# Sub-layer ends of a two-layer diffusion trunk: gate products and whole-tile splits on VectorE, two weight blocks of the first attention head in other tiles

## The chip, the core and the metric

One core of one Trainium2 chip runs the whole program. The metric is the device time of one execution in microseconds, lower is better. In the core, TensorE (PE) multiplies matrices, VectorE (DVE) and ScalarE (ACT) work on tiles of 128 partitions, GpSimd (POOL) does a few small or side operations, and SyncE (SP) issues the transfers. Each engine works through its own list of instructions in order and waits on semaphores for the others.

## The reference

A trunk of two layers on 256 context tokens and 512 latent tokens of width 1024. Each layer is a half-step SwiGLU FFN, a token mixer and another half-step FFN; layer 0 mixes by differential attention, layer 1 by grouped-query attention. Every one of these six sub-layers reads a normalised and modulated stream and adds its gated, normalised result back:

```python
def modulated_norm(h, g, m, k):
    return rmsnorm(h, g) * (1.0 + m[..., k + 1, :]) + m[..., k, :]

def gated_residual(h, y, g, m, k, weight):
    return h + weight * m[..., k + 2, :] * rmsnorm(y, g)

def half_ffn(h, m, k, g_pre, g_post, w_in, w_out):
    y = swiglu(modulated_norm(h, g_pre, m, k), w_in, w_out)
    return gated_residual(h, y, g_post, m, k, 0.5)
```

All is in float32. The output is the latent stream, 512 x 1024.

## The kernel before

**Numbers.** A float32 operand of TensorE is split into a high part `hi` (a cast on ScalarE) and a low part `lo = x - hi` (on VectorE), and a product is three matmuls: high-high, high-low, low-high. Activations live as `uh` and `ul` (high and low, transposed, the stationary operand), weights as `wh` and `wl`.

**Tiles.** The 768 tokens are six tiles of 128 tokens: 0 and 1 are context, 2 to 5 latent. `ys[t]` is the working tile of one token tile, 128 x 1024 in SBUF.

**The six sub-layers** run one after another: FFN (0,0) to about 545 us, differential attention to 1060, FFN (0,1) to 1540, FFN (1,0) to 2070, grouped attention to 2360, FFN (1,1) (latent tiles alone) to the end. Between two of them stands a sub-layer end: the last group of an output projection is summed tile by tile, and each finished tile is turned into the next sub-layer's input. I number the ends 1 to 6; ends 1, 3 and 4 close the FFNs (0,0), (0,1) and (1,0), ends 2 and 5 the two attentions, end 6 the kernel. The FFN ends work on six tiles, with five operands left for the last group: 30 matmuls a tile in two halves of 512 columns.

**One tile of an end** (class `Finish`) goes through: the sum from PSUM into `y` (`add_y`, L414, VectorE, once a half); the gate product `yg = y * gate` (`gated`, L369, GpSimd, once a half: half 0 from `half`, half 1 from `chain`); the sum of squares of `y` (L267, ScalarE); its inverse root on GpSimd (`rms`, two operations of 128 x 1, L97 and L99); `h = yg * r + h` (L382, VectorE), whose store is queued on SyncE; the sum of squares of `h` (L267) and its root (L97, L99); `y = h * r` (L388, VectorE); eight transposes on TensorE into `pre_t` (L280); the modulation back into `y` (L294 on VectorE, L290 on ScalarE, four pieces each); and the split, `split_u`: the cast `uh` on ScalarE (L310), then `ul = y - uh`. The table `WIDE` names 13 tiles over the first four ends that are split whole; there the low part is two halves of 128 x 512, one on VectorE (L315) and one on GpSimd (L316). All other tiles are split in two steps, each with its low half on VectorE (L318). At the attention ends `yg` and `h` are weight tiles, so the product reads there as `wh<-y,g` and `h` as `wl<-wh,rms,wl`.

**Order.** At the FFN ends the order of VectorE, ScalarE and GpSimd is the order in which `w_out_last` writes it (`ordered()`, with the table `LAGS` of how many halves each step of a tile trails the projection); on TensorE, and at the attention ends, a scheduler sets it, fed by the strings `DA_SLOT_END` and `GA_SLOT_END`. `marks` holds the last ACT, DVE and POOL instruction of a split or a root, and `behind` keeps the next FFN's loads of weights behind them.

**The first attention head.** Head 0 of differential attention needs eight k-blocks of `w_in`, loaded two by two by `block` (L846), cast (L849) and split (L852) into six `wh` and six `wl` weight tiles (`wtile`). At end 1 the output projection still holds five of the six. A block that is `kept` goes instead into two tiles of the tag `pl` (four buffers, idle there); before, that holds for the first block of heads 1, 3, 5 and 7.

Of the kernel before, what the change touches and what calls it, by code (L numbers as in the profile page):

```python
# [13 lines left out]
ALU = mybir.AluOpType  # L14
# [7 lines left out]
KC = D // P  # L22
# [32 lines left out]
def raw(ap):  # L55
    return ap.bitcast(F32)
# [3 lines left out]
def trunk(ctx: ExitStack, tc: tile.TileContext, a: dict, out: bass.AP):  # L60
    nc = tc.nc
# [44 lines left out]
    def stage():  # L106
        return wp.tile([P, 1024], F32, tag="stage", name="stage", bufs=NSTAGE)

    def wtile(which):
        return wp.tile([P, 1024], F32R, tag="w" + which, name="w" + which, bufs=6)  # L110
# [36 lines left out]
    marks = {}  # L147
# [155 lines left out]
    def split_u(t, place, parts):  # L303
        i, j = place
        u32 = ys[t].rearrange("p (k q) -> p k q", k=KC)
        n = KC // parts
        for k in range(0, KC, n):
            ks = slice(k, k + n)
            hi, lo = (x[:, i, ks, j * P : (j + 1) * P] for x in (uh, ul))
            marks["act"] = nc.scalar.copy(hi, u32[:, ks])  # L310
            if parts == 1:
                yield
            if parts == 1:
                m = KC // 2
                marks["dve"] = nc.vector.tensor_tensor(out=lo[:, :m], in0=u32[:, :m], in1=raw(hi[:, :m]), op=ALU.subtract)  # L315
                marks["pool"] = nc.gpsimd.tensor_tensor(out=lo[:, m:], in0=u32[:, m:], in1=raw(hi[:, m:]), op=ALU.subtract)  # L316
            else:
                marks["dve"] = nc.vector.tensor_tensor(out=lo, in0=u32[:, ks], in1=raw(hi), op=ALU.subtract)  # L318

    def load_gate(l, s):  # L320
        g = []
# [31 lines left out]
    class Finish:  # L353
# [10 lines left out]
        def gated(self, t, dh):  # L364

            if dh == 0:
                self.yg = self.tile()
            cols = slice(512 * dh, 512 * dh + 512)
            nc.gpsimd.tensor_tensor(  # L369
                out=self.yg[:, cols], in0=ys[t][:, cols], in1=self.gate[1 if t < CT else 0][:, cols], op=ALU.mult  # L370
            )

        def chain(self, t):
            i, j = self.place[t]
            cols = slice(j * P, (j + 1) * P)
            h = load_h(t, self.first, self.tile if self.s == 1 else None)
            ss = sumsq(ys[t], uh[:, i, :, cols])
            self.gated(t, 1)
            yg = self.yg
            r = rms(ss)  # L380
            yield
            nc.vector.scalar_tensor_tensor(out=h, in0=yg, scalar=r, in1=h, op0=ALU.mult, op1=ALU.add)  # L382
            nc.sync.dma_start(out=hd[t] if self.nxt else out[0, (t - CT) * P : (t - CT + 1) * P], in_=h)
            if not self.nxt:
                return
            r = rms(sumsq(h, ys[t]))
            yield
            nc.vector.tensor_scalar(out=ys[t], in0=h, scalar1=r, scalar2=None, op0=ALU.mult)  # L388
            yield
            pts = turn(t, t in self.wide)  # L390
            modulate(*self.nxt, t, [pts[k // 4][:, (k % 4) * P : (k % 4 + 1) * P] for k in range(KC)])
            yield
            yield from split_u(t, self.place[t], 1 if t in self.wide else 2)
# [416 lines left out]
    def diff_attention(ctx, place, fin):  # L810
# [22 lines left out]
        def block(n, parts, use, kept=False):  # L833


            def half(which):
                if kept:
                    return ep.tile([P, 768], F32R, tag="pl", name="w" + which, bufs=4)
                return wtile(which)[:, :n]

            st = stage()[:, :n]
            for cols, src in parts:
                dst = st[:, cols]
                if len(src.shape) == 3:
                    dst = dst.rearrange("p (c f) -> p c f", f=P)
                nc.sync.dma_start(out=dst, in_=src)  # L846
            yield
            hi = half("h")
            nc.scalar.copy(hi, st)  # L849
            yield  # L850
            lo = half("l")
            nc.vector.tensor_tensor(out=lo, in0=st, in1=raw(hi), op=ALU.subtract)  # L852
            use(hi, lo)
            yield

        class Head:
# [3 lines left out]
            def blocks(self):  # L860
                def use(k, hi, lo):
                    for i in range(2):
                        self.ws[k + i] = hi[:, i * 384 : (i + 1) * 384], lo[:, i * 384 : (i + 1) * 384]

                for k in range(0, KC, 2):
                    parts = [(slice(i * 384, (i + 1) * 384), w_in[:, k + i, :, self.h, :]) for i in range(2)]
                    yield block(768, parts, partial(use, k), k == 0 and self.h % 2)

            def open(self):
                self.q = {}  # L870
# [888 lines left out]
```

## Time and profile before

| what | before |
|---|---|
| time, median of 3 runs | 2739.59 us |
| lowest and highest run | 2735.0 and 2741.33 us |
| the profiled execution, own time | 2744.38 us |
| its span in the trace | 2742.6 us |
| mean granted TensorE clock, share of full speed | 0.988 |
| PE matmuls busy | 2639.0 us (96%) |
| DVE busy | 2016.4 us (74%) |
| ACT busy | 1135.7 us (41%) |
| POOL busy | 357.6 us (13%) |

The profiled execution is 4.8 us above the median and 1.8 us above its own span. "Busy" is the time in which an engine executes; matmuls are pipelined, so the ends of TensorE's rows are modelled. A row of a timeline begins with start and duration, and ends with the engine's idle time before the instruction and what released it.

### The profile page before, as it was taken

Reading aid. Unit: us, or ns where it says so; the run is one execution under the profiler, and the core shown is the slowest. Engines: PE = TensorE matmul, PEld = TensorE weight load, DVE = VectorE, ACT = ScalarE, POOL = GpSimd, SP = SyncE. Lnnn points to the kernel's source line nnn. Section 1 sums busy time; section 2 is a strip of 40 time slices with the busy share of each in tenths; the row PEclk is TensorE's granted clock in tenths of the full one; section 3 lists DMA queues with packets and bytes.
Section 4 is the critical chain, followed back from the end, with each engine's and each line's share of the span. In section 5 each row is a group of like instructions: output and inputs, shape, how many; then the busy total and the mean of one; then the engine's idle time right before and its main releaser. Section 6 shows DMA issues by size and latency. Waiting matters only on the chain.

```text
span 2742.6 us, 38868 instructions
## 1 busy us (share of the span) xinstructions
PE 2639.0 (96%) x14720; PEld 2404.6 (88%) x14720; DVE 2016.4 (74%) x3052; ACT 1135.7 (41%) x2323; POOL 357.6 (13%) x643
## 2 busy tenths in 40 slices
PE   6999999989999998999999999999999999899998
PEld 5999998879999987999988789999787899788887
DVE  4988879867777787888788689787766778733355
ACT  4333333156666665333342353333324554622232
POOL 0000000054333343000000310000004210200001
PEclk9999999999999999999999999999999999999999
DMA  7444457531111113444375334344743211444452
GB/s 229 136 132 151 142 170 254 167 122 45 38 32 49 54 63 97 134 124 139 117 251 175 123 104 154 125 137 155 282 141 131 79 39 39 149 142 139 149 166 89
DMA packets 301860, 354.13 MB, mean 129 GB/s; under 512 B 15808, under 2 KB 234088, under 8 KB 301672
## 3 DMA queue, kind: packets, MB, share of 16 engines
q1 hardware_dynamic: 301672, 351.64, 39.9%
q8 instruction: 116, 1.90, 0.3%
q14 instruction: 72, 0.59, 0.1%
HBM read 303.05 MB, written 48.54 MB: 128 GB/s over the span
## 4 chain that ended last, share of the span: by engine, by line
PE 75%; DVE 9%; ACT 5%; issue 5%; POOL 3%; DMA 2%; POOLq 0%; DVEq 0%; ACTq 0%; SPq 0%
PE y_ps L423 23%; PE ff_p L615 15%; PE ff_ps L615 12%; PE ff_ps L735 8%; PE qkv_ps L806 5%; PE ff_ps L477 2%; PE ff_ps L767 1%; DVE h L382 1%; PE S L984 1%; DVE wl L104 1%; PE o_ps L1056 1%; ACT y L267 1%; PE kv_ps L806 1%; PE q_ps L806 1%; PE o_ps L1428 1%
## 5 line engine op out<-in xcount | busy, mean ns | idle before, releaser
L423 PE MATMUL y_ps<-wh,gx 128*128 128x512 f32 x1936 | 604.5, 391 | 1.5 <-ACT wh L103 1.5
L423 PEld LDWEIGHTS y_ps<-wh,gx 128*128 128x128 f32 x1936 | 363.2, 188 | 81.1 <-ACT wh L103 2.9
L103 ACT CAST wh<-stage 128x1024 fp32r<-128x1024 f32 x224 | 232.1, 1048 | 434.7 <-PE y_ps L423 217.0
L423 PE MATMUL y_ps<-wl,gx 128*128 128x512 f32 x968 | 377.3, 390 | 0.5 <-DVE wl L104 0.4
L104 DVE TENSOR_TENSOR wl<-stage,wh 128x1024 fp32r<-128x1024 f32 x224 | 273.2, 1224 | 96.3 <-ACT wh L103 94.4
L414 DVE TENSOR_TENSOR y<-y_ps,y 128x512 f32<-128x512 f32 x324 | 221.3, 686 | 109.3 <-PE y_ps L423 107.7
L369 POOL TENSOR_TENSOR yg<-y,g 128x512 f32<-128x512 f32 x44 | 58.3, 1326 | 1820.3 <-DVE y L414 1818.1
L185 DVE SCALAR_TENSOR_TENSOR acc<-stage,scond,acc 128x1024 f32<-128x1024 f32 x196 | 244.1, 1277 | 30.3 <-DMA stage<-in_ada_w 30.2
L615 PE MATMUL ff_p<-t,wh 128*128 128x384 f32 x960 | 244.4, 335 | 1.5 <-ACT sil L568 1.5
L103 ACT CAST wh<-raw 128x1024 fp32r<-128x1024 f32 x120 | 120.1, 1049 | 255.9 <-DVE raw L594 255.9
L423 PEld LDWEIGHTS y_ps<-wl,gx 128*128 128x128 f32 x968 | 181.8, 188 | 38.5 <-DVE wl L104 1.6
L615 PEld LDWEIGHTS ff_p<-t,wh 128*128 128x128 f32 x960 | 173.8, 188 | 1.8 <-ACT sil L568 1.8
L615 PE MATMUL ff_p<-t,wl 128*128 128x384 f32 x480 | 161.0, 335 | 2.9 <-DVE wl L104 2.9
L615 PE MATMUL ff_ps<-uh,wh 128*128 128x384 f32 x480 | 160.9, 335 | 1.7 <-DVE two L637 1.7
L615 PE MATMUL ff_ps<-uh,wl 128*128 128x384 f32 x480 | 160.4, 334 | 0.0
L615 PE MATMUL ff_ps<-ul,wh 128*128 128x384 f32 x480 | 160.3, 334 | 0.0
L104 DVE TENSOR_TENSOR wl<-raw,wh 128x1024 fp32r<-128x1024 f32 x120 | 141.2, 1218 | 0.0
L806 PE MATMUL qkv_ps<-wh,uh 128*128 128x384 f32 x384 | 136.9, 357 | 4.1 <-ACT wh L849 2.7
L806 PE MATMUL qkv_ps<-wl,uh 128*128 128x384 f32 x384 | 129.8, 338 | 2.5 <-DVE wl L852 2.5
L615 PE MATMUL ff_p<-uh,u 128*128 128x384 f32 x480 | 132.1, 336 | 0.0
L806 PE MATMUL qkv_ps<-wh,ul 128*128 128x384 f32 x384 | 129.9, 338 | 0.1
L615 PE MATMUL ff_ps<-t,wh 128*128 128x384 f32 x480 | 124.6, 340 | 2.2 <-ACT one L633 1.9
(250 smaller groups left out, 6356.4 us busy)
## 6 DMA issues: line engine op xcount, KB each, us to landing
stage<-in_ffn_w_in SPq DMA_DIRECT2D x176, 512.0 KB
stage<-in_ada_w SPq DMA_DIRECT2D x136, 512.0 KB
stage<-in_ffn_w_out SPq DMA_DIRECT2D x88, 512.0 KB
gd<-g SPq DMA_DIRECT2D x66, 384.0 KB
gr<-gd SPq DMA_DIRECT2D x57, 384.0 KB
stage<-in_da_w_in SPq DMA_DIRECT2D x64, 192.0 KB
hd<-h SPq DMA_DIRECT2D x18, 512.0 KB
h<-hd SPq DMA_DIRECT2D x16, 512.0 KB
```

Source lines behind the costliest of these rows:

```text
L103: nc.scalar.copy(hi, src)
L104: nc.vector.tensor_tensor(out=lo, in0=src, in1=raw(hi), op=ALU.subtract)
L185: nc.vector.scalar_tensor_tensor(out=acc[c], in0=st, scalar=scond[:, k, c : c + 1], in1=acc[c], op0=ALU.mult, op1=ALU.add)
L267: nc.scalar.activation(junk, src, AF.Square, accum_out=ss)
L369: nc.gpsimd.tensor_tensor(out=self.yg[:, cols], in0=ys[t][:, cols], in1=self.gate[1 if t < CT else 0][:, cols], op=ALU.mult)
L382: nc.vector.scalar_tensor_tensor(out=h, in0=yg, scalar=r, in1=h, op0=ALU.mult, op1=ALU.add)
L414: nc.vector.tensor_tensor(out=y, in0=ps, in1=y, op=ALU.add)
L423: nc.tensor.matmul(ps, lhsT=x, rhs=w, start=(i == 0), stop=(i == n - 1))
L477: nc.tensor.matmul(ps, lhsT=ww[:, k, :], rhs=moving(uu, k, two), start=(k == 0 and n == 0), stop=(k == KC - 1 and n == 2),)
L615: nc.tensor.matmul(ps[:, :hw], lhsT=ww[:, k * P : (k + 1) * P], rhs=bb[:, k, cols], start=(first and k == 0 and n == 0), stop=(last and k ...
L735: nc.tensor.matmul(ps[:, :nt], lhsT=ww[:, k, :], rhs=uu[:, :, k, cols], start=(k == 0 and n == 0), stop=(k == KC - 1 and n == 2),)
L806: nc.tensor.matmul(ps[:, :n], lhsT=x, rhs=w, start=(k == 0 and m == 0), stop=(k == KC - 1 and m == 2))
```

## The change

Three things. The gate product `yg = y * gate` moves from GpSimd to VectorE, in all six ends (64 products of 128 x 512: 44 at the FFN ends, 20 at the attention ends). The low part of the 13 tiles that are split whole becomes one VectorE operation of 128 x 1024 in place of a half on VectorE and a half on GpSimd. And the first two blocks of head 0's `w_in` (k = 0 and k = 2, which hold k-blocks 0 to 3) become `kept`: they go into the four `pl` tiles, so that the third and the fourth block take the weight tiles that the first and the second had. The arithmetic is the same.

```diff
@@ split_u
-            if parts == 1:
-                m = KC // 2
-                marks["dve"] = nc.vector.tensor_tensor(out=lo[:, :m], in0=u32[:, :m], in1=raw(hi[:, :m]), op=ALU.subtract)
-                marks["pool"] = nc.gpsimd.tensor_tensor(out=lo[:, m:], in0=u32[:, m:], in1=raw(hi[:, m:]), op=ALU.subtract)
-            else:
-                marks["dve"] = nc.vector.tensor_tensor(out=lo, in0=u32[:, ks], in1=raw(hi), op=ALU.subtract)
+            marks["dve"] = nc.vector.tensor_tensor(out=lo, in0=u32[:, ks], in1=raw(hi), op=ALU.subtract)
@@ Finish.gated
-            nc.gpsimd.tensor_tensor(
+            nc.vector.tensor_tensor(
                 out=self.yg[:, cols], in0=ys[t][:, cols], in1=self.gate[1 if t < CT else 0][:, cols], op=ALU.mult
             )
@@ Head.blocks
-                    yield block(768, parts, partial(use, k), k == 0 and self.h % 2)
+                    yield block(768, parts, partial(use, k), k == 0 and self.h % 2 or k < 4 and self.h == 0)
```

The changed file is five lines shorter, so its line numbers are five lower from `load_gate` on (the product is L364 there, `add_y` L409, `h` L377, `y = h * r` L383, the split L313, the weight cast L844).

VectorE at end 3, one tile of the loop and the start of the next, before:

```order
L388 TENSOR_SCALAR y_103<-h,rms 128x1024
L414 TENSOR_TENSOR y_104<-y_ps,y_104 128x512
L315 TENSOR_TENSOR ul<-y_102,uh 128x4x128
L382 SCALAR_TENSOR_TENSOR h<-yg,rms,h 128x1024
L414 TENSOR_TENSOR y_105<-y_ps,y_105 128x512
L294 TENSOR_SCALAR y_103<-pre_t,ab_14976,ab_14316 128x128 x4
L388 TENSOR_SCALAR y_104<-h,rms 128x1024
```

and now:

```order
L409 TENSOR_TENSOR y_104<-y_ps,y_104 128x512
L364 TENSOR_TENSOR yg<-y_104,g_15576 128x512
L313 TENSOR_TENSOR ul<-y_102,uh 128x8x128
L377 SCALAR_TENSOR_TENSOR h<-yg,rms,h 128x1024
L409 TENSOR_TENSOR y_105<-y_ps,y_105 128x512
L364 TENSOR_TENSOR yg<-y_105,g_15576 128x512
L294 TENSOR_SCALAR y_103<-pre_t,ab_14971,ab_14311 128x128 x4
L383 TENSOR_SCALAR y_104<-h,rms 128x1024
```

Each sum of a half is now followed by its product, the split covers the whole tile, and nothing else changed places in the loop.

ScalarE where end 1 begins (`gx` and `wh` of L103 are the FFN's last operands, L849 or L844 the casts of head 0's blocks), before:

```order
L103 CAST gx<-gr 128x768
L103 CAST wh<-stage 128x1024
L849 CAST wh<-stage 128x768
L267 ACTIVATE uh,ss<-y_101 128x8x128
L267 ACTIVATE y_101,ss<-h 128x1024
```

and now:

```order
L103 CAST gx<-gr 128x768
L844 CAST wh<-stage 128x768
L103 CAST wh<-stage 128x1024
L844 CAST wh<-stage 128x768 x2
L267 ACTIVATE uh,ss<-y_101 128x8x128
L267 ACTIVATE y_101,ss<-h 128x1024
```

Three of head 0's four blocks are cast ahead of the first tile's sum of squares, where one was.

VectorE at end 5 (`neg`, `r` and `e` are steps of the attention's last units, y_103 is tile 2), before:

```order
L414 TENSOR_TENSOR y_103<-y_ps,y_103 128x512 x2
L1420 TENSOR_TENSOR pt<-p_t,pt 128x3x128 x2
L1389 TENSOR_REDUCE neg<-S 128x1
L382 SCALAR_TENSOR_TENSOR wl<-wh,rms,wl 128x1024
```

and now:

```order
L409 TENSOR_TENSOR y_103<-y_ps,y_103 128x512
L364 TENSOR_TENSOR wh<-y_103,g_23266 128x512
L409 TENSOR_TENSOR y_103<-y_ps,y_103 128x512
L1415 TENSOR_TENSOR pt<-p_t,pt 128x3x128
L364 TENSOR_TENSOR wh<-y_103,g_23266 128x512
L1415 TENSOR_TENSOR pt<-p_t,pt 128x3x128
L377 SCALAR_TENSOR_TENSOR wl<-wh,rms,wl 128x1024
L1384 TENSOR_REDUCE neg<-S 128x1
```

The scheduler has put two products among the attention's own work, and the maximum of a unit's scores (`neg`) behind `h` of tile 2.

## Rows read from the trace of the kernel before

**Rows 1.** The chain of work that ended last, shares of the span by engine:

```profile
PE 75%; DVE 9%; ACT 5%; issue 5%; POOL 3%; DMA 2%; POOLq 0%; DVEq 0%; ACTq 0%; SPq 0%
```

**Rows 2.** TensorE's waits, 525 to 640 us (total, times, longest, in us):

```profile
PE k_t L934 <- POOL ks L927: 3.0, 2, 2.1
PE qkv_ps L806 <- ACT wh L849: 2.7, 1, 2.7
PE qkv_ps L806 <- DVE wl L852: 2.5, 1, 2.5
PE pre_t L280 <- DVE y L388: 2.3, 2, 1.7
```

**Rows 3.** TensorE's waits, 1535 to 1612 us:

```profile
PE pre_t L280 <- DVE y L388: 2.8, 3, 1.7
```

**Rows 4.** TensorE's waits, 2055 to 2160 us:

```profile
PE k_t L1338 <- DVE xn L1286: 3.2, 1, 3.2
PE kv_ps L806 <- DVE wl L104: 2.6, 1, 2.6
```

**Rows 5.** TensorE's waits, 980 to 1085 us:

```profile
PE q_t L1081 <- DVE o L1078: 5.7, 3, 3.0
```

**Rows 6.** TensorE's waits, 2280 to 2400 us:

```profile
PE pre_t L280 <- DVE y L388: 3.5, 3, 1.3
PE ff_ps L477 <- DVE ul L318: 2.3, 1, 2.3
```

**Rows 7.** TensorE's timeline at end 1, the transposes of tiles 2 and 3:

```profile
571.11 1.09 PE L280 MATMUL pre_t<-ident,y 128*128 128x128 f32 x8 [0.54 <-DVE y L388]
...
580.77 1.09 PE L280 MATMUL pre_t<-ident,y 128*128 128x128 f32 x8 [1.74 <-DVE y L388]
```

**Rows 8.** VectorE's timeline at end 1:

```profile
547.92 1.29 DVE L382 SCALAR_TENSOR_TENSOR h<-yg,rms,h 128x1024 f32<-128x1024 f32 x1 [2.25 <-POOL rms L99]
...
564.72 2.31 DVE L382 SCALAR_TENSOR_TENSOR h<-yg,rms,h 128x1024 f32<-128x1024 f32 x1
...
569.28 1.77 DVE L388 TENSOR_SCALAR y<-h,rms 128x1024 f32<-128x1024 f32 x1 [0.36 <-POOL rms L99]
...
573.81 0.69 DVE L315 TENSOR_TENSOR ul<-y,uh 128x512 fp32r<-128x512 f32 x1 [2.16 <-ACT uh L310]
...
583.97 0.99 DVE L817 TENSOR_TENSOR lam<-lam 128x128 f32<-128x128 f32 x1 [2.65 <-DMA lam<-in_da_lambda]
...
601.36 0.75 DVE L388 TENSOR_SCALAR y<-h,rms 128x1024 f32<-128x1024 f32 x1 [0.77 <-POOL rms L99]
```

**Rows 9.** GpSimd's timeline at end 1:

```profile
564.16 1.80 POOL L316 TENSOR_TENSOR ul<-y,uh 128x512 fp32r<-128x512 f32 x1
...
568.37 0.22 POOL L97 TENSOR_SCALAR ms<-ss 128x1 f32<-128x1 f32 x1 [2.41 <-ACT y L267]
...
569.21 1.29 POOL L369 TENSOR_TENSOR yg<-y,g 128x512 f32<-128x512 f32 x1
...
594.64 0.93 POOL L97 TENSOR_SCALAR ms<-ss 128x1 f32<-128x1 f32 x1
```

**Rows 10.** VectorE by line and shape (busy us, mean ns | idle before, releaser):

```profile
L104 DVE TENSOR_TENSOR wl<-stage,wh 128x1024 fp32r<-128x1024 f32 x224 | 273.2, 1224 | 96.3 <-ACT wh L103 94.4
...
L382 DVE SCALAR_TENSOR_TENSOR h<-yg,rms,h 128x1024 f32<-128x1024 f32 x22 | 39.5, 1797 | 23.5 <-POOL rms L99 23.5
...
L388 DVE TENSOR_SCALAR y<-h,rms 128x1024 f32<-128x1024 f32 x18 | 28.7, 1594 | 13.1 <-POOL rms L99 13.1
...
L382 DVE SCALAR_TENSOR_TENSOR wl<-wh,rms,wl 128x1024 f32<-128x1024 f32 x10 | 12.8, 1279 | 4.2 <-POOL rms L99 4.2
...
L506 DVE TENSOR_TENSOR y<-y,y 128x512 f32<-128x512 f32 x9 | 6.1, 683 | 0.0
```

**Rows 11.** The last tile's `h` at end 3, VectorE's timeline:

```profile
1592.33 2.30 DVE L382 SCALAR_TENSOR_TENSOR h<-yg,rms,h 128x1024 f32<-128x1024 f32 x1
```

**Rows 12.** Busy us of each engine in a stretch of end 2 (PE, PEld, DVE, ACT, POOL):

```profile
960.00:1060.00 100.00, 86.00 (x497) 74.75 (x495) 81.89 (x154) 64.22 (x176) 50.49 (x88) 0.95 0.21 69
```

## The prediction

> **What bounds the kernel now.** The chain of waits comes first: three quarters of the span is TensorE's own work [rows 1], and the change touches none of it. So all that it can move is time in which TensorE stands still, and the next view is the list of TensorE's waits around each of the six ends. Each has the same picture: TensorE waits a few times for a tile on its way back from the sum to the next sub-layer's operand, or for that sub-layer's first weights. At the FFN ends (1, 3, 4) two waits of the transposes for `y = h * r` stand first (0.54 and 1.74 us at end 1 [rows 7]; at end 3 the same pair and one more, 2.8 us in all, 1.7 the longest [rows 3]); end 1 goes on with 2.7 us for a cast, 2.5 us for its low part and 2.1 us for the transposes of the first keys [rows 2]; end 4 with 2.6 us for a low part and 3.2 us for the keys [rows 4]. At the attention ends the waits hang on other steps: 5.7 us at end 2 on `o` of the last units [rows 5], 3.5 and 2.3 us at end 5 [rows 6]. End 6 has no such wait and one tile after another; there the product of a half runs beside ScalarE's sum of squares.
>
> Third, the timelines of VectorE and GpSimd at end 1, side by side. The same `h` takes 1.29 us at 547.92 and 2.31 us at 564.72 [rows 8], and beside the second runs GpSimd's half of a split, 564.16 to 565.96 [rows 9]: VectorE gets nowhere until GpSimd is through. The same holds for `y = h * r`: 1.77 us at 569.28 beside a product that began at 569.21, and 0.75 us at 601.36 with GpSimd idle [rows 8, 9]. Over the whole run the 22 `h` of the FFN ends and the tail average 1.80 us, the ten of the attention ends 1.28; the 18 `y` average 1.59 [rows 10]. So (1.80 - 1.28) x 22 = 11.4 us and (1.59 - 0.75) x 18 = 15.1 us of VectorE's time are such blocking, nearly all of it at ends 1, 3 and 4.
>
> **The FFN loop, step by step.** A tile there takes VectorE 9.66 us: the distance of the two transposes in [rows 7], of which TensorE itself needs 9.66 - 1.74 = 7.92. The loop runs sum, ScalarE's sum of squares and cast, low half, `h`, sum of squares, root, `y`, next sum. With nothing large left on GpSimd, `h` gives back 2.31 - 1.29 = 1.02 us and `y` 1.77 - 0.75 = 1.02. The split grows from a half (0.69 us [rows 8]) to a whole tile, for which the weight split of the same size stands, 1.22 us [rows 10]: +0.53. The two products cost VectorE 0.68 us each by the nearest row, a sum of two SBUF operands of 128 x 512 [rows 10]. The second starts when the sum is done and ends inside ScalarE's sum of squares of the same tile and its cast, for which VectorE now waits 2.16 us ahead of the split [rows 8]; the first lies between the sum of half 0 and the modulation, where VectorE has 0.36 us idle ahead of `y` [rows 8], so at most 0.68 - 0.36 = 0.32 of it shows. If the 2.16 us were not there, the pair would cost 1.36 a tile. New loop: 9.66 - 1.02 - 1.02 + 0.53 = 8.15 us, up to 8.5 with the 0.32. That is 0.2 to 0.6 over TensorE's 7.92. The first wait is 0.54 where the second is 1.74, so TensorE comes to it with 1.2 us in hand, which covers two to five such tiles: both transpose waits go, 2.3 us at each of the three ends.
>
> What is late next is the last tile. Its `h` is reached through three loops, three times -1.51, and is itself blocked (2.30 us at end 3 [rows 11]), another -1.0:
>
> End 3: -4.5 - 1.0 = **-5.5** us, taken from the last pair of tiles, for which the next FFN waits. All of TensorE's waits there end on this chain or go before it; -3.5 if the 0.32 and the sub-layer's first weights hold it, -6.5 if all of them vanish.
>
> End 4: two plain loops -3.0; in the last one the second product, a root step and VectorE's weight splits hold each other as at end 1 (a root's first step takes 0.93 us at 594.64 and 0.22 at 568.37 [rows 9]), which I put at -2.5; `h` -1.0; the keys' chain hangs on it. **-6.5**, from -4 to -8.5. The wait for the keys (3.2 us) stays in part, because TensorE gets there earlier too.
>
> End 1: loops into tiles 3 and 4, -3.0; the wait of VectorE for `lam` (2.65 us [rows 8]) does not shrink, since its transfer is queued on SyncE behind the store of an `h` that itself comes earlier; tile 4's `y` -1.0, tile 5's `h` -1.0, and the roots beside weight splits -1: **-6**. The new places of the weights matter here. In TensorE's order the first projections wait for the cast and the low part of head 0's second block, 2.7 + 2.5 us [rows 2]: these two blocks now lie in `pl` tiles and are cast ahead of tile 0's sum of squares, the third takes the one free weight tile. Those waits go whatever the loop does, but TensorE then runs on into the first key transposes, which need ScalarE to evacuate the first projection behind the sum of squares of tile 5's `h`. So the weights alone only move the wait, and the sum is what the last `h` gains. -3 if ScalarE's casts of the later blocks hold that `h`'s sum of squares, -9 if all waits of [rows 2] but the last go. The extra loads ahead of the first stores on SyncE are two blocks of 384 KB, early in a stretch with no transfer wait but `lam`; nothing.
>
> End 2: VectorE is busy 81.9 of 100 us [rows 12], the product is pure work there (the ten `h` of the attention ends are not blocked, 1.28 us [rows 10]). Twelve tiles' halves x 0.68 = 8.2 us come on VectorE; in return the roots of the attention's `o`, which hang behind products on GpSimd, come earlier, and that is the wait of 5.7 us [rows 5]. **-1**, from -4 to +2. End 5: eight halves x 0.68 = 5.4 us, the maximum of a unit's scores stands behind `h` of tile 2, 1.3 us later, against transposes and low parts freed of GpSimd's product [rows 6]: **+0.5**, from -3 to +2.5. End 6: 0.
>
> The Trainium skill, "Perfetto Trace Analysis", section Optimizing Scalar/DVE Operations, speaks for the other direction: when VectorE is saturated, work may be offloaded, even to GpSimd, though it "might not help" between these two. By it, end 2 would lose the 8.2 us of products in place of gaining 1; the trace at the FFN ends agrees with its reservation (2.31 against 1.29 us).
>
> **Sum.** -6 - 1 - 5.5 - 6.5 + 0.5 = -18.5, against the profiled execution's own 2744.4: 2725.9. That execution lies 4.8 above the median of the runs shown, so about 2721 on the scale of the median, 0.7% faster.
>
> **Rivals.**
> A, *only the loop waits go.* The three pairs of transpose waits vanish (2.3 + 2.3 + 2.3 = 6.9 us) and all that follows is caught by the next late thing: `lam` and ScalarE's queue at end 1, the keys at end 4, the first weights at end 3. For it: TensorE arrives earlier everywhere. Against: the keys' and the last pair's chains run through the very `h` and `y` that get shorter. With ends 2 and 5 at zero: 2739.6 - 6.9 = 2733.
>
> B, *VectorE becomes the bound at the attention ends*, slower than before. 20 products x 0.68 = 13.7 us go to an engine that is busy 82% there, in stretches in which its low parts and scores release TensorE. It decides if half of that or more lands on TensorE's waits at ends 2 and 5 and the FFN ends fare as in A, or worse, because products on VectorE now block GpSimd's roots (0.93 for 0.22 us, twice a tile, 0.7 x 2 x 4 tiles = 5.7 us at an end). With all 13.7 lost and 6.9 gained: 2739.6 + 6.8 = 2746.
> The Trainium skill, "SBUF — State Buffer", section Who interferes with whom, gives the lock behind this: an operation of VectorE with two SBUF inputs and a GpSimd operation that reads SBUF exclude each other, whoever issues first; by it a root can wait for a product of VectorE as `h` did for one of GpSimd, and the 0.93 us row is of that kind.
>
> C, *all waits at the FFN ends go*, with the stretches at half clock behind them: to the upper ends above, -9 - 4 - 6.5 - 8.5 - 3 = -31, 2709.
>
> D, *the weights' places backfire.* The four `pl` tiles are wanted again by head 1's first block and by the units of head 0; if head 1's block waits for the last projection of head 0, its cast comes too late for the next head. Price: one wait like the 2.7 + 2.5 us of [rows 2], +5 on the forecast: 2726.
>
> **How the numbers follow.** Forecast 0.62, C 0.08 (toward 2709), D 0.08 (2726), A 0.15 (2733), B 0.07 (2746). This kernel's measurement tells about 0.2%, 5.5 us, from no change: 2734.1 to 2745.1. Forecast, C and D are faster by more; A is faster in two cases of three, 0.10 against 0.05 within; B's 0.07 is split, 0.03 within and 0.04 slower. That makes 0.88, 0.08 and 0.04. The range leaves out C's far end and B: 2708 to 2734, the sums of the bounds (-31, and -3 + 2 - 3.5 - 4 + 2.5 = -6).
>
> **What would show it.** Right: every `h` at 1.28 and every `y` at 0.75 us in the loop, products of 0.68 us inside VectorE's wait for `uh`, no transpose wait at ends 1, 3 and 4, no wait for `wh` and `wl` at end 1, and a key wait there that is larger than before. Wrong: loops still above 9 us; roots on GpSimd near 1 us; TensorE's waits at ends 2 and 5 grown by more than 3 us each; a new wait for weights near 630 us, in head 1.

## The result and the profile after

| what | before | after |
|---|---|---|
| time, median | 2739.86 us | 2724.23 us |
| lowest and highest run | 2735.0, 2742.32 us | 2722.72, 2726.1 us |
| ratio, 95% interval | | 0.9941, 0.9931 to 0.9952 |
| the profiled execution, own time | 2744.38 us | 2724.36 us |
| its span | 2742.6 us | 2722.6 us |

The change is 15.6 us faster by the medians. The profiled pair differs by 20.0 us, more than the medians do; why is told below. The busy times of the page after:

```profile
PE 2632.1 (97%) x14720; PEld 2401.8 (88%) x14720; DVE 2026.2 (74%) x3116; ACT 1135.0 (42%) x2323; POOL 252.9 (9%) x566
```

GpSimd lost 105 us of work and VectorE gained only 10, though 44 us of products came to it: 26.5 us came back from `h` (39.5 to 28.2) and `y` (28.7 to 13.5). The rows by line and shape answer [rows 10] (busy us, mean ns of one | idle before, releaser):

```profile
L364 DVE TENSOR_TENSOR yg<-y,g 128x512 f32<-128x512 f32 x44 | 30.4, 692 | 1.3
L377 DVE SCALAR_TENSOR_TENSOR h<-yg,rms,h 128x1024 f32<-128x1024 f32 x22 | 28.2, 1282 | 15.9 <-POOL rms L99 15.9
...
L364 DVE TENSOR_TENSOR wh<-y,g 128x512 f32<-128x512 f32 x20 | 13.6, 685 | 0.1
L383 DVE TENSOR_SCALAR y<-h,rms 128x1024 f32<-128x1024 f32 x18 | 13.5, 749 | 6.5 <-POOL rms L99 6.5
```

`h` fell from 1797 to 1282 ns and `y` from 1594 to 749: nothing blocks them any more. TensorE's waits after, first end 1 (505 to 640 us), against [rows 2]:

```profile
PE k_t L929 <- POOL ks L922: 7.6, 2, 6.7
```

End 3 (1515 to 1612 us), against [rows 3]:

```profile
PE pre_t L280 <- DVE y L383: 1.8, 2, 1.1
```

End 4 (2035 to 2160 us), against [rows 4]:

```profile
PE k_t L1333 <- DVE xn L1281: 6.3, 1, 6.3
```

End 5 (2260 to 2400 us), against [rows 6]:

```profile
PE p_t L1403 <- DVE r L1394: 3.6, 1, 3.6
PE pre_t L280 <- DVE y L383: 3.5, 2, 2.5
```

The waits of the loop are gone at ends 1 and 4, and one wait for the keys holds most of what is left. At end 5 there is a wait that was not there before, 3.6 us for `r`.

**Shift by end.** How much an end gained is read from two traces: an instruction in the middle of a stage starts earlier by so much, and what the shift grows by from one stage to the next belongs to the end between them. Ahead of end 1 and behind it, before and then after:

```profile
518.29 0.69 DVE L414 TENSOR_TENSOR y<-y_ps,y 128x512 f32<-128x512 f32 x1 [0.41 <-PE y_ps L423]
...
704.04 0.90 ACT L1004 ACTIVATE e<-S,neg 128x768 f32<-128x768 f32 x1
```

```profile
517.14 0.69 DVE L409 TENSOR_TENSOR y<-y_ps,y 128x512 f32<-128x512 f32 x1 [0.41 <-PE y_ps L418]
...
697.93 0.90 ACT L999 ACTIVATE e<-S,neg 128x768 f32<-128x768 f32 x1
```

518.29 - 517.14 = 1.15 and 704.04 - 697.93 = 6.11: end 1 gained about 5. In the table each number is the median over 30 to 160 such pairs in a stage, always against the same trace of before; negative is earlier, in us. The kernels of the experiments stand in it too.

| kernel | end 1 | end 2 | end 3 | end 4 | end 5 | median time |
|---|---|---|---|---|---|---|
| before, a second trace | -0.1 | -1.1 | -0.3 | +0.1 | +0.1 | 2740.3 (1 run) |
| after | -5.1 | -2.0 | -7.1 | -8.4 | +3.8 | 2724.2 |
| after, a second trace | -3.9 | -1.3 | -6.5 | -8.6 | +3.8 | 2724.5 |
| split_only | -2.2 | -4.1 | -1.7 | -4.0 | +0.5 | 2731.9 |
| products_only | -3.3 | -0.1 | -4.2 | -5.6 | +3.4 | 2729.4 |
| blocks_only | +2.9 | -3.3 | -0.9 | -1.0 | +1.0 | 2740.3 |
| no_blocks | -4.6 | +0.5 | -6.5 | -7.7 | +1.3 | 2725.3 |
| end5_gpsimd | -4.2 | -1.7 | -6.5 | -8.4 | +0.8 | 2723.6 |
| end5_tile2 | -4.6 | -0.6 | -6.5 | -8.6 | +1.0 | 2722.8 |
| end2_gpsimd | -5.3 | -1.9 | -6.6 | -8.4 | +3.7 | 2722.9 |
| lam_later | -5.6 | -2.1 | -7.2 | -8.0 | +2.3 | 2723.2 |
| last_half_h | -7.0 | +1.1 | -5.5 | -9.6 | +2.2 | 2723.9 |
| combo2_h | -6.4 | -3.2 | -7.0 | -9.6 | -2.2 | 2718.4 |

The medians of before beside them lie between 2739.6 and 2740.5. The profiled execution of before is 4.5 us above its median of 2739.86 and that of after lies at its own, which is why the pair shows 20.0 and the medians 15.6. The second trace of before, near the median, shows where: it is 2.6 us earlier ahead of end 1 and 1.1 at end 2. Against that trace the ends of the changed kernel gain 17.5 us, not 18.8.

The column of end 3 holds more than end 3. Up to 1840 us the changed kernel has gained 5.9 us there, in both of its traces; the rest of the 7.1 and 6.5 comes near 1900 us, in the middle of FFN (1,0), where TensorE waits once for a weight. Before:

```profile
PE y_ps L423 <- ACT wh L103: 1.2, 1, 1.2
```

The changed kernel has no such wait in one trace and 0.6 us in the other.

### The profile page after: what moved, and what is told of

Same layout as the page of the kernel before. It is cut to its first block, busy times and chain, and to the rows that moved or that the text cites. A ratio compares the mean times of both kernels' runs of the same rounds, so it can differ in the third digit from the quotient of the medians.

```text
span 2722.6 us, 38903 instructions
## 1 busy us (share of the span) xinstructions
PE 2632.1 (97%) x14720; PEld 2401.8 (88%) x14720; DVE 2026.2 (74%) x3116; ACT 1135.0 (42%) x2323; POOL 252.9 (9%) x566
## 4 chain that ended last, share of the span: by engine, by line
issue 74%; PE 16%; DVE 4%; POOL 3%; ACT 3%; DMA 0%; POOLq 0%; DVEq 0%; ACTq 0%
PE qkv_ps L801 6%; PE y_ps L418 3%; PE S L979 1%; POOL rms L99 1%; PE o_ps L1051 1%; PE kv_ps L801 1%; PE q_ps L801 1%; PE o_ps L1423 1%; POOL ms L97 1%; ACT e L999 1%; PE S L1379 1%; POOL rs L91 1%; PE p_t L1031 1%; PE p_t L1403 0%; DMA h<-in_x 0%
## 5 line engine op out<-in xcount | busy, mean ns | idle before, releaser
L103 ACT CAST wh<-stage 128x1024 fp32r<-128x1024 f32 x224 | 232.3, 1049 | 427.7 <-PE y_ps L418 206.2
L409 DVE TENSOR_TENSOR y<-y_ps,y 128x512 f32<-128x512 f32 x324 | 222.1, 688 | 99.8 <-PE y_ps L418 98.3
L103 ACT CAST wh<-raw 128x1024 fp32r<-128x1024 f32 x120 | 120.1, 1049 | 256.5 <-DVE raw L589 256.5
L97 POOL TENSOR_SCALAR ms<-ss 128x1 f32<-128x1 f32 x66 | 22.8, 345 | 2050.8 <-ACT uh L267 1917.5
```

What stands on the lines that cost most here:

```text
L97: nc.gpsimd.tensor_scalar(out=ms, in0=ss, scalar1=D * EPS, scalar2=None, op0=ALU.add)
L103: nc.scalar.copy(hi, src)
L409: nc.vector.tensor_tensor(out=y, in0=ps, in1=y, op=ALU.add)
```

## The experiments

### The two halves of the change on GpSimd's work, one at a time

`split_only` is the kernel before with the whole-tile split alone:

```diff
...
-                m = KC // 2
-                marks["dve"] = nc.vector.tensor_tensor(out=lo[:, :m], ...)
-                marks["pool"] = nc.gpsimd.tensor_tensor(out=lo[:, m:], ...)
+            marks["dve"] = nc.vector.tensor_tensor(out=lo, in0=u32[:, ks], in1=raw(hi), op=ALU.subtract)
```

(The `if` and `else` around these lines go; tiles split in two steps keep their line.)

> The kernel before, with the whole-tile split on VectorE alone; products stay on GpSimd. Blocking theory: h is freed (1.28 us instead of 2.31 in the FFN loop), y = h * r stays blocked (1.77), the split costs 1.22 instead of 0.69, so a loop of 9.66 us becomes about 9.2. Shift of the trace by end: end 1 -2.5, end 3 -2.5, end 4 -3, ends 2 and 5 within 0.3 of zero; in all about -8 us, 2732. Rival, that what counts is how much is taken from GpSimd's list: 22 of the 108 us that left it would give about a fifth of the gain, -4.

`products_only` is the kernel before with the products alone:

```diff
-            nc.gpsimd.tensor_tensor(
+            nc.vector.tensor_tensor(
                 out=self.yg[:, cols], in0=ys[t][:, cols], in1=self.gate[...][:, cols], op=ALU.mult
...
```

> The kernel before, with the gate products on VectorE; the split stays in two halves. Blocking theory: y is freed (0.75), h stays blocked (2.31), loop about 8.6 us. End 1 -4, end 2 -2, end 3 -3, end 4 -4.5, end 5 +3.8 as in the changed kernel, in all about -10 us, 2730. Rival by the share of GpSimd's work: four fifths of the gain at the FFN ends, -16 there.

Measured: 2731.9 us, ratio 0.9969 (0.9957 to 0.9980), and 2729.4 us, 0.9962 (0.9949 to 0.9975), both times as expected. VectorE by line and shape, `split_only` and then `products_only`:

```profile
L383 DVE TENSOR_SCALAR y<-h,rms 128x1024 f32<-128x1024 f32 x18 | 28.8, 1598 | 13.6 <-POOL rms L99 13.6
L377 DVE SCALAR_TENSOR_TENSOR h<-yg,rms,h 128x1024 f32<-128x1024 f32 x22 | 28.2, 1282 | 23.8 <-POOL rms L99 23.8
```

```profile
L382 DVE SCALAR_TENSOR_TENSOR h<-yg,rms,h 128x1024 f32<-128x1024 f32 x22 | 39.5, 1797 | 16.3 <-POOL rms L99 16.3
L388 DVE TENSOR_SCALAR y<-h,rms 128x1024 f32<-128x1024 f32 x18 | 13.4, 746 | 5.6 <-POOL rms L99 5.6
```

Each part frees exactly the operation that it stood beside and leaves the other blocked: without GpSimd's half of the split `h` takes 1282 ns and `y` still 1598, without its products `y` takes 746 and `h` still 1797. At the three FFN ends the split gives 2.2 + 1.7 + 4.0 = 7.9 us and the products 3.3 + 4.2 + 5.6 = 13.1; both without the blocks give 4.6 + 6.5 + 7.7 = 18.8. The halves nearly add, 21.0 against 18.8. The rival, by the share of GpSimd's work, had put 4 and 16. So it is who stands beside whom that counts, more than how much GpSimd has to do. The -4.1 of `split_only` at end 2, where I had expected less than 0.3, is taken up below.

### The blocks, alone and left out

`blocks_only` has only the third part of the change, `no_blocks` all but it:

```diff
-                    yield block(768, parts, partial(use, k), k == 0 and self.h % 2)
+                    yield block(768, parts, partial(use, k), k == 0 and self.h % 2 or k < 4 and self.h == 0)
```

> The kernel before, with two blocks of head 0 in the pl tiles and nothing else. Theory, that the weights alone only move the wait: the waits for cast and low part (2.7 and 2.5 us) go, the wait for the first key transposes grows from 2.1 to about 7, end 1 within 0 to -1.5, no other end moves; 2738 to 2740. Rival, that the weights were the bound: end 1 -4 to -5, 2735.

> The changed kernel without the blocks in the pl tiles. Theory: end 1 loses 0 to 2 us against the changed kernel (its last h is what counts), the waits for cast and low part are back and the key wait is short; all other ends as in the changed kernel: 2724 to 2726. Rival, that the weights were the bound of end 1: +4 to +5, 2728 to 2729.

Measured: 2740.3 us, ratio 1.0002 (0.9993 to 1.0012), and 2725.3 us, 0.9942 (0.9925 to 0.9959). TensorE's waits from 525 to 640 us with the blocks alone, and below without them:

```profile
PE k_t L934 <- POOL ks L927: 5.9, 2, 5.1
...
PE qkv_ps L806 <- DVE wl L852: 2.5, 1, 2.5
PE qkv_ps L806 <- ACT wh L849: 0.6, 1, 0.6
```

```profile
PE k_t L929 <- POOL ks L922: 4.9, 2, 4.1
PE qkv_ps L801 <- DVE wl L847: 1.1, 2, 0.6
...
```

Alone, the blocks shorten the wait for a cast from 2.7 to 0.6 us, and the wait for the keys grows from 3.0 to 5.9 [rows 2]: the wait moves, and nothing is gained. I had expected both weight waits to go; the one for the low part stays at 2.5 us, and end 1 of this trace is even 2.9 us longer. Without the blocks, the waits for weights are only 1.1 us, which fits that they hung on the same loop; the keys wait 4.9 us there, where I had expected a short wait. The blocks bring nothing that these runs can tell from zero, alone or with the rest.

### The products at end 5

`end5_gpsimd` is the changed kernel with all eight products of end 5 back on GpSimd, `end5_tile2`, shown here, with only the two of tile 2:

```diff
-            nc.vector.tensor_tensor(
+            (nc.gpsimd if (self.l, self.s) == (1, 1) and t == CT else nc.vector).tensor_tensor(
```

> The changed kernel with the products of end 5 back on GpSimd. Order theory: the loss at end 5 comes from the scheduler's order, in which the maximum of a unit's scores stands behind h of tile 2; with the old order TensorE's wait of 3.6 us for r is gone and end 5 is back near the kernel before: 2 to 3.5 us less than the changed kernel, 2721 to 2723. Rival, that end 5's loss is only the clock (0.84 to 0.93 there in the changed kernel): no difference, 2724 to 2725.

> The changed kernel with only tile 2's two products of end 5 back on GpSimd; that alone puts the maximum ahead of h of tile 2 again. Order theory: the wait of 3.6 us for r is gone as with all eight products moved back, 2721 to 2723. Rival, that the load of eight products on VectorE is what costs: a quarter of the loss comes back, 1 us, 2723.5 to 2724.5, and the wait for r stays over 2.5 us.

Measured: 2723.6 us and 2722.8 us, ratios 0.9941 (0.9929 to 0.9954) and 0.9936 (0.9923 to 0.9950). VectorE's timeline of the changed kernel there, and TensorE's first transposes behind it:

```profile
2317.93 1.28 DVE L377 SCALAR_TENSOR_TENSOR wl<-wh,rms,wl 128x1024 f32<-128x1024 f32 x1 [0.77 <-POOL rms L99]
2319.13 0.95 DVE L1384 TENSOR_REDUCE neg<-S 128x1 f32<-128x768 f32 x1
...
```

```profile
2323.08 1.20 PE L1403 MATMUL p_t<-ident,e 128*128 128x128 f32 x5 [3.60 <-DVE r L1394]
```

and of `end5_tile2`, with its wait at that place:

```profile
2317.71 0.95 DVE L1384 TENSOR_REDUCE neg<-S 128x1 f32<-128x768 f32 x1
2319.17 1.28 DVE L377 SCALAR_TENSOR_TENSOR wl<-wh,rms,wl 128x1024 f32<-128x1024 f32 x1 [0.51 <-POOL rms L99]
```

```profile
PE p_t L1403 <- DVE e L1395: 0.8, 1, 0.8
```

With the maximum ahead of `h` the wait is 0.8 instead of 3.6 us, although six of the eight products are still VectorE's. So the wait hangs on the order, not on the load. In the traces end 5 drops from +3.8 to +1.0; the medians gain 0.6 to 1.7 us, which is inside what the runs scatter.

Part of that drop is TensorE's granted clock, the other explanation that I had named beforehand. Here are 140 us around end 5 at the same place in each trace (PE, PEld, DVE, ACT, POOL busy, granted clock): the changed kernel, `no_blocks`, `lam_later` (a run below) and `end5_tile2`. The first three have the changed kernel's wait of 3.6 us for `r`.

```profile
2256.20:2396.20 140.00, 128.69 (x795) 116.35 (x794) 100.62 (x180) 72.50 (x157) 10.81 (x22) 0.95 0.34 106
```

```profile
2259.00:2399.00 140.00, 128.21 (x805) 115.23 (x805) 100.72 (x181) 73.00 (x158) 10.84 (x22) 0.98 0.35 110
```

```profile
2256.35:2396.35 140.00, 128.41 (x801) 115.51 (x800) 100.59 (x180) 72.40 (x157) 10.81 (x22) 0.96 0.36 109
```

```profile
2257.40:2397.40 140.00, 129.96 (x807) 116.58 (x806) 99.77 (x179) 73.31 (x158) 13.40 (x24) 0.96 0.36 110
```

With the changed kernel's wait, end 5 stands at +3.8 where TensorE got 0.95 of its clock, at +2.3 with 0.96 and at +1.3 with 0.98. Without it, `end5_tile2` stands at +1.0 with 0.96, `end5_gpsimd` at +0.8 with 0.98, and the kernel before at 0 with 0.98. So at an equal clock the order costs 0.5 to 1.3 us; the rest of the 3.8 goes with the clock. Whether the wait for `r` itself brings the clock down stays open: six of the seven traces with that wait have 0.95 or 0.96, the five with all products of end 5 on GpSimd 0.98 or 0.99.

### The products at end 2

```diff
+            (nc.gpsimd if (self.l, self.s) == (0, 1) else nc.vector).tensor_tensor(
```

> The changed kernel with the products of end 2 back on GpSimd. Theory, that end 2 gains because the roots of o no longer queue behind products: the wait of 5.7 us on o is back (1.3 in the changed kernel), other waits of end 2 shrink by about 4, and the time is 0 to 2 us above the changed kernel, 2724 to 2726.5. Rival, that the products burden VectorE there: 2 us below, 2722.

Measured: 2722.9 us, ratio 0.9938 (0.9925 to 0.9950). TensorE's waits from 980 to 1085 us, the changed kernel and below it this one:

```profile
PE ff_ps L472 <- DVE wl L104: 4.3, 2, 2.4
PE ff_ps L472 <- ACT wh L103: 2.9, 2, 2.7
...
PE q_t L1076 <- DVE o L1073: 1.3, 1, 1.3
```

```profile
PE q_t L1076 <- DVE o L1073: 5.7, 3, 3.0
PE ff_ps L472 <- DVE wl L104: 3.4, 1, 3.4
```

The wait for `o` does come and go with the products, 5.7 against 1.3 us, as the theory says. But what it gives up is taken by the first weights of the next FFN (4.3 + 2.9 against 3.4), and the shift of end 2 is -1.9 here and -2.0 in the changed kernel. No gain and no loss can be told; the time lies below the 2724 to 2726.5 that I had expected.

### The kernels before and after, a second time

> The changed kernel once more, instruction for instruction, to see how far a single trace can be trusted: the waits by name and their lengths the same within 0.1 us, the shift of an end against the earlier trace of the same kernel up to 1 us at the FFN ends, and up to 2.5 us at ends 2 and 5, where the granted clock fell to 0.8 or 0.9 in some traces of one and the same order and not in others. Time 2724 to 2725.

> The kernel before once more, for a second trace to hold the ends of the others against. If end 2 of the changed kernel is really 1 to 2 us shorter, this trace keeps end 2 within 1 us of the first; the rival is that end 2 moves by 2 to 4 us from trace to trace of one and the same order, as the trace with only the blocks moved suggests (-3.3 there, with nothing changed at end 2), and then nothing below that is to be told at end 2. FFN ends within 1 us of the first trace.

Measured: 2724.5 us, ratio 0.9941 (0.9929 to 0.9954); one run of before, 2740.3 us. By name and length its waits at the ends are those of the first trace within 0.4 us, and its end 1 differs by 1.2; I had put 0.1 and 1. End 2 moved by 1.1 us between the two traces of before, and `blocks_only`, with nothing changed at end 2, `split_only`, with one tile's split changed there, and `no_blocks`, with end 2 as in the changed kernel, stand at -3.3, -4.1 and +0.5. A shift of 2 us at end 2 is no finding.

### What is late next

`lam_later` is the changed kernel with VectorE's steps on `lam` behind the last `y` of end 1 (`scaled[0]` is that instruction). The transfer of `lam` and ScalarE's exponential, whose table load takes 1.28 us in the loop of the changed kernel, stand later with them:

```diff
+        with tc.issue_after(scaled[0].ins):
+            lp = lam[:, 4:6]
+            nc.vector.tensor_tensor(out=lp, in0=lam[:, 0:4:2, :], in1=lam[:, 1:4:2, :], op=ALU.mult)
...
```

> The changed kernel with VectorE's work on lam, for which it waits 2.3 us in the loop of end 1, put behind the last tile's y. Theory, that the last h of end 1 sets its length: the key wait of 6.7 us falls to about 4 and end 1 is 2 to 3 us shorter, 2721 to 2723. Rival, that ScalarE's casts of late weight transfers hold the keys: no difference, 2724 to 2725.

`last_half_h` puts the last tile's second sum and its `h` first:

```diff
-                stages(2 * (t - start) + dh)
+                e = 2 * (t - start) + dh
+                if t < tiles[-1]:
+                    stages(e)
+                elif dh:
+                    stages(e - 1)
+                    if stage_of[t] == 1 and t in coming:
+                        step(t)
+                    stages(e)
```

> The changed kernel with another order at the end of the FFN ends: the last tile's second sum stands ahead of tile 4's scaling and tile 3's modulation on VectorE, and its h ahead of tile 3's split. Theory, that after the change the last h is what the next sub-layer waits for: the key waits of 6.7 and 6.3 us at ends 1 and 4 shrink by 2 to 3 each (at end 1 the wait for lam and late weight casts keep the rest), end 3 has only 2.2 us of waits left and gives 1 at most; in all -6, 2717 to 2720. Rival, that the keys hang on ScalarE's casts: under 2 us in all, 2722.5 or more.

`combo2_h` is both, `end5_tile2`, and the casts of the next head behind the last `y` of end 1:

```diff
-        whole(3)
+        with tc.issue_after(scaled[0].ins):
+            whole(3)
```

> The changed kernel with all that the runs so far point to: the last tile's sum and h first, lam and the next head's casts behind the last y of end 1, tile 2's products of end 5 on GpSimd. If the parts add: end 1 -4.5, end 3 -1, end 4 -3, end 5 -1.5 against the changed kernel, 2714 (2711 to 2717). Rival, that TensorE's granted clock takes back what the waits give: 2718 or more.

Measured: 2723.2 us, ratio 0.9940 (0.9927 to 0.9952); 2723.9 us, 0.9934 (0.9922 to 0.9946); 2718.4 us, 0.9923 (0.9909 to 0.9936). The wait for the keys at end 1, in that order:

```profile
PE k_t L919 <- POOL ks L912: 5.9, 2, 5.1
```

```profile
PE k_t L936 <- POOL ks L929: 5.7, 2, 4.9
```

```profile
PE k_t L926 <- POOL ks L919: 5.3, 2, 4.4
```

They take 1.6 to 2.3 us off the changed kernel's longest wait of 6.7; for each of the first two I had put 2 to 3. The shift of end 1 is -5.6, -7.0 and -6.4, against -5.1 and -3.9 in the changed kernel. ScalarE in `lam_later` shows a part of what holds the rest: a cast that waits for its transfer, ahead of the sum of squares of the last `h`.

```profile
590.92 0.83 ACT L834 CAST wh<-stage 128x768 fp32r<-128x768 f32 x1 [1.50 <-DMA stage<-in_da_w_in]
591.66 1.05 ACT L267 ACTIVATE y<-h 128x1024 f32<-128x1024 f32 x1
```

That `h` ends at 591.14 (589.86 and 1.28), so the cast costs 0.5 us; no run takes the other 4.6 apart.

The time of `last_half_h` is the rival's, under 2 us in all, though ends 1 and 4 do gain in its trace (-7.0 and -9.6, against -5.1 and -8.4). At end 3, where tile 4's `y` now stands behind tile 5's sum and product, the new order makes a wait of its own:

```profile
PE pre_t L280 <- DVE y L383: 2.8, 1, 2.8
```

against 1.8 us in the changed kernel. `combo2_h` has the lowest median of all kernels here, 6 us below the changed one; its interval and the changed kernel's overlap (0.9936 and 0.9931). It misses the 2711 to 2717 that I had expected and lies where the rival had it, that the clock takes back what the waits give. Its trace cannot show that: it is of the fastest run (2713.9), and its -2.2 at end 5, with the order of `end5_tile2`, goes with a clock of 0.99 against 0.96.

## Why the prediction was right, point by point

The time, 2724.2, lies in the range, 3 us above the 2721 that was forecast.

**The blocking.** Right, and shown by the two halves: `h` 1282 and `y` 749 ns, products 692.

**The loop.** Put at 8.15 to 8.5 us; VectorE's timeline of the changed kernel at end 1, two tiles of it:

```profile
561.84 1.22 DVE L313 TENSOR_TENSOR ul<-y,uh 128x1024 fp32r<-128x1024 f32 x1 [1.62 <-ACT uh L310]
562.98 1.28 DVE L377 SCALAR_TENSOR_TENSOR h<-yg,rms,h 128x1024 f32<-128x1024 f32 x1
...
566.79 0.75 DVE L383 TENSOR_SCALAR y<-h,rms 128x1024 f32<-128x1024 f32 x1
...
570.49 1.23 DVE L313 TENSOR_TENSOR ul<-y,uh 128x1024 fp32r<-128x1024 f32 x1 [1.63 <-ACT uh L310]
571.63 1.28 DVE L377 SCALAR_TENSOR_TENSOR h<-yg,rms,h 128x1024 f32<-128x1024 f32 x1
...
579.84 0.29 DVE L812 TENSOR_TENSOR lam<-lam 128x128 f32<-128x128 f32 x1 [2.34 <-DMA lam<-in_da_lambda]
```

571.63 - 562.98 = 8.65 us, 0.15 over the upper bound: of the 0.36 us that VectorE idled ahead of `y` nothing is left, so the first product shows, as the 0.32 said. The second hides in the wait for `uh`, 1.62 now where it was 2.16. All transpose waits at ends 1 and 4 are gone, and at end 3 1.8 of 2.8 us remain, where none was to.

**End 1, -6.** The first key transposes start at 603.54 before and 596.48 after; less the 1.15 of the opening that is -5.9. Behind them the end gives back 0.8, and over the two traces it is -5.1 and -3.9. The wait for `lam` stayed (2.65 and 2.34 us), and the blocks alone gave nothing, both as put. That the two waits for weights go "whatever the loop does" was wrong: with the blocks alone 2.5 us stay, and the loop without the blocks leaves only 1.1. And the bound of -9 does not follow from [rows 2]: without the keys the waits there add up to 7.5.

**End 3, -5.5.** Right: -5.9 up to 1840 us, in both traces; only with the wait near 1900 does the table's -7.1 pass the bound of -6.5. The last `h`, to be held against [rows 11]:

```profile
1579.70 1.28 DVE L377 SCALAR_TENSOR_TENSOR h<-yg,rms,h 128x1024 f32<-128x1024 f32 x1
```

It starts 12.63 us earlier, of which 8.26 had been gained by then: -4.4, where three loops were put at -4.5. TensorE's waits at this end, 6.3 us in all before, are 2.2 after. The rest of the gain fits its clock, which the sum had left out. In the 20 us around the last tile it was granted 0.91 before and 1.00 after, which is 1.8 us by an estimate from these two rows:

```profile
1580.00:1600.00 20.00, 16.58 (x113) 15.46 (x112) 14.32 (x21) 10.19 (x20) 9.31 (x13) 0.91 0.31 107
```

```profile
1565.50:1585.50 20.00, 18.19 (x130) 16.70 (x129) 15.91 (x26) 12.71 (x26) 3.71 (x8) 1.00 0.31 106
```

**End 4, -6.5**, measured -8.4 and -8.6, at the bound of -8.5. The keys of end 4, before and after:

```profile
2129.90 0.45 PE L1338 MATMUL k_t<-ident,xn 128*128 128x128 f32 x1 [3.21 <-DVE xn L1286]
```

```profile
2107.86 0.45 PE L1333 MATMUL k_t<-ident,xn 128*128 128x128 f32 x1 [6.26 <-DVE xn L1281]
```

22.04 us earlier, of which 15.39 had been gained by then: -6.65, the step as it was worked out. Its parts were not: the last `h` starts 4.5 us earlier, where 5.5 had been put, and the way from it to `y` is 2.2 shorter, where 1.0 had been put. The other 1.8 us come behind the keys. In the same 20 us (2130.00 to 2150.00 before, 2107.96 to 2127.96 after) TensorE was granted 0.86 of its clock before and 0.91 after, by the same estimate 1.0 us, and two of its waits there shrink from 2.3 to 1.7 us.

**End 2, -1**: not to be told from zero. The step on the roots is right (5.7 to 1.3 us), but I had not asked what is late next there, as I had at the FFN ends.

**End 5, +0.5**, bound +2.5: measured +3.8 twice. This is the term that was mis-sized. I had read the order, and priced the maximum's place at the 1.3 us of `h` and set it against gains; but the row of `h` brings its own wait for a root with it, two maxima then run back to back behind it, and `r` and `e` of both units follow them, so that TensorE waits 3.6 us. That wait replaces others: all of TensorE's waits at this end grow from 9.7 to 11.3 us, and at the clock of before (0.98) the same order stands at +1.3, inside the bounds. What takes it past them is the clock of 0.95, which the sum had left out here too.

**Sum.** Ends -5.1 - 2.0 - 7.1 - 8.4 + 3.8 = -18.8 in the profiled pair, forecast -18.5; -16.5 in the second trace, and -15.6 by the medians. Gains at ends 3 and 4 and the loss at end 5 made up for each other, and in all three a part is TensorE's clock, up there and down here. That the sum comes so near is partly luck; the blocking and the loop are no luck.

**The rivals.** A (the waits only move, -6.9): at end 1 most of the wait did turn up at the keys, but earlier, and the time is 9 us below A's 2733. B: its mechanism is real at one place. At end 4 a root's first step, GpSimd's timeline of the changed kernel, and VectorE beside it:

```profile
2098.75 2.88 POOL L97 TENSOR_SCALAR ms<-ss 128x1 f32<-128x1 f32 x1 [3.21 <-ACT uh L267]
```

```profile
2098.06 2.36 DVE L104 TENSOR_TENSOR wl<-stage,wh 128x1024 fp32r<-128x1024 f32 x2
...
2100.33 1.22 DVE L313 TENSOR_TENSOR ul<-y,uh 128x1024 fp32r<-128x1024 f32 x1
```

All over the run, though, the 66 such steps average 345 ns after and 325 before (22.8 against 21.5 us): 1.3 us, not 5.7 an end; and ends 2 and 5 together lost 1.8 us, not 13.7. C: the waits at the FFN ends did not all go; the keys still wait 6.7 and 6.3 us. D: no wait for weights near 630 us.

## What to carry to other kernels

Look at the operations of two engines that stand beside each other, not at the engines' totals: here a product of 1.3 us on GpSimd, busy 13%, made the `y` beside it on VectorE 1.0 us longer, 15 times of 18, on the chain that mattered. Price an end by following the last tile through it, and ask at every end what is late next; and where a scheduler has put a step behind another, price the wait that this other step brings with it, not its duration alone. Before an end of one trace is held against that of another, compare the granted clock.

## What I had not expected

A step of 0.22 us on GpSimd took 2.88 us, while VectorE ran three operations with two SBUF inputs one behind the other (2098.06 to 2101.55): it started 0.7 us into the first and was not let in between them. "The Trainium skill", page SBUF — State Buffer, section Who interferes with whom, has the one that issues first block the other; the row agrees, and shows in addition that back-to-back operations kept the smaller one out for all three.

And the granted clock of one and the same order differs from trace to trace: 0.95, 0.96 and 0.98 over the 140 us at end 5 above, with +3.8, +2.3 and +1.3 us there. These 2.5 us are as much as most of the experiments at that end were to tell.
